# Attention in two layers: score products of 128 rows throughout, two units per step, the sink as a column, keys and queries laid out by their loads

## Chip, cores and metric

The kernel runs on one core of one Trainium2 chip. The metric is device time in microseconds of one execution; a verdict compares medians of runs on the same chip. Before the change the median of three runs is 3075.5 us (3071.46 to 3081.49).

## What is computed

Two transformer layers over 1024 latent tokens and 256 context tokens of width 1024, in float32. Layer 0 mixes tokens by a Fourier transform in half its channels and by windowed attention with a sink in the other half (8 query heads, 2 key heads). Layer 1 is attention over neighbourhoods of a grid with a learned bias (16 heads). Each ends with a SwiGLU layer. Cut to the attention:

```python
def _window_attention(q, k, v, k_ctx, v_ctx, sink):
    s_win = jnp.einsum('bnqkgd,bnjkd->bnkgqj', qb, kw).astype(jnp.float32) * scale
    s_ctx = jnp.einsum('bnqkgd,bjkd->bnkgqj', qb, k_ctx).astype(jnp.float32) * scale
    s_win = jnp.where(mask[None, :, None, None], s_win, NEG)
    p = jax.nn.softmax(jnp.concatenate([s_win, s_ctx, sk], axis=-1), axis=-1).astype(v.dtype)
    o = (jnp.einsum('bnkgqj,bnjkd->bnqkgd', p[..., :nw], vw)
         + jnp.einsum('bnkgqj,bjkd->bnqkgd', p[..., nw:nw + C], v_ctx))
...
def one_row(r):          # layer 1
    s_nb = jnp.einsum('bqhd,bjhd->bhqj', q_row, k_rows).astype(jnp.float32) * scale + bias[None]
    s_nb = jnp.where(mask[None, None], s_nb, NEG)
    s_cx = jnp.einsum('bqhd,bjhd->bhqj', q_row, k_ctx).astype(jnp.float32) * scale
    p = jax.nn.softmax(jnp.concatenate([s_nb, s_cx], axis=-1), axis=-1).astype(v.dtype)
```

`sk` is the sink: one more score per head that enters the sum of the softmax and has no value.

## The kernel before

Products that need float32 accuracy are made of parts: an operand is `hi` + `lo`, two numbers of TensorE's reduced float32 type, and a product is three matmuls (`mm3`, lines 74 to 76). The dense layers are long runs of those.

The attention of both layers goes by **units**: 128 queries of one head with up to 640 keys (three blocks of 128 in the window, two of context), 80 units in layer 0 and 128 in layer 1. The class `Unit` has the steps of one:

- `scores`: a head has 64 features, so a query's `hi` and `lo` are stacked into 128 rows, `q_st`. For each of two runs of keys one product takes `q_st` with `k_st`, the keys' high parts written twice, one in each half of the rows (line 658). A second takes the 64 rows of the queries' high parts with the keys' low parts `k_l` (line 659). The sums go into a two-bank PSUM tile `s_ps`, of which there are two.
- `maxima` (line 592, on DVE): bias or mask added, the maximum taken, `s_ps` read out into `sm`.
- `exponents` (line 598, on ACT): `pr` = exp, with its sum. In layer 0 a second exponential (line 601) makes the sink's part and POOL adds it (line 602).
- `normalise`: the reciprocal on DVE (line 606), the product with it on POOL (line 607).
- `turn` (line 615): TensorE transposes `pr` by blocks of 128 into PSUM banks `pt_ps`; DVE copies the first run of keys out (line 621), ACT the second (line 619).

`values` (lines 714 and 1181) multiplies turned probabilities with the values, each of two heads in 64 columns of the array, into `po`; ACT and DVE `split` the result into `o_hi`, `o_lo` in layer 0 (lines 720, 722) or `h_hi`, `h_lo` in layer 1 (lines 1188, 1190).

`pipeline` writes these steps in a skewed order, a unit at a time: scores of unit i, turn of unit i − 3 or i − 4, the exponential and normalisation of unit i − 1, the maximum of unit i, then values of an earlier pair in four or three parts. In layer 1 that order is binding for PE, DVE, ACT and POOL; in layer 0 a scheduler arranges the instructions from it. Ahead of units in layer 0 stand the steps of `ada_third` (line 149: a 1 MB load of `ada_w` and four products, 40 times), which make later layers' modulation vectors, and `load_q0`, which loads and turns a tile of queries; in layer 1 loads of the next pair of heads and the addition of masks to the bias tables.

In layer 1 keys and queries come from DRAM, where `turn_qk` put them while the in-projection ran: keys in three arrays (high parts twice for each head of a pair, low parts), queries in two. `load_part` (line 1120) brings a pair's keys and queries in on POOL's DMA queue and values on SP's. In layer 0 `turn_keys` (lines 488 to 496) builds `kA`, `kB` (high parts, twice) and `kL` (low parts) in SBUF during the Fourier mixing. Loads and stores on one engine's queue are issued in the order in which they are written.

Of the kernel before, what the change touches and what calls it, by code (L numbers as in the profile page):

```python
# [16 lines left out]
P = 128  # L17
D = 1024
KT = D // P
# [14 lines left out]
class Pools:  # L34
    """Tile pools opened and closed by hand, so that lifetimes need not nest in the source."""
# [20 lines left out]
def bc(ap, axis, n):  # L56
    """The AP with a dimension of stride 0 put in at `axis`."""
    ap = ap.unsqueeze(axis)
    shape = list(ap.shape)
    shape[axis] = n  # L60
    return ap.broadcast_to(shape)


def build(tc, io):
# [7 lines left out]
    def mm3(out, lh, ll, rh, rl, first, last):  # L72
        """out += l^T r with both operands as exact sums of two float32r parts."""
        TE.matmul(out, lh, rh, start=first, stop=False)  # L74
        TE.matmul(out, lh, rl, start=False, stop=False)  # L75
        TE.matmul(out, ll, rh, start=False, stop=last)  # L76

    def rsqrt_into(r, v, tmp):
        """r = v ** -0.5: a table's value and one Newton step."""
# [6 lines left out]
    # ------------------------------------------------------------------ constants  # L86
# [82 lines left out]
    # ------------------------------------------------------------------ DRAM scratch  # L169
# [4 lines left out]
    q1_d = tc.dram_tile([P, 8, 2, 8, P], F32, name="q1_d")  # L174
# [28 lines left out]
    def modulate(hi, lo, x, r, a, b, wk, n, perm=None, shaped=lambda t: t):  # L203
        """hi + lo = x * r * a + b; `perm` reads the tokens in another order."""
# [6 lines left out]
    # ------------------------------------------------------------------ layer 0: in-projection  # L211
# [26 lines left out]
    def rstd0(c, x):  # L238
        """Steps to the roots of a chunk."""
# [38 lines left out]
    # the first chunk takes the modulation vectors and the weights as they arrive  # L278
# [98 lines left out]
    for c in range(T // CH):  # L377
        h_hi, h_lo = hs[c]

        for u in range(CH // P):  # L380
# [10 lines left out]
            if j == NT - 1:  # L391
                # the room of the inputs and of their norms is free for the Fourier mixing
# [19 lines left out]
            # rotation  # L412
# [17 lines left out]
            # queries: (hi | lo) of a pair's first head, (lo | hi) of its second  # L430
# [28 lines left out]
    # twiddle columns: of l1 = 0 and 4 (cos | -sin), 1..3 (cos | -sin | -cos), context 0, 1 (cos | -sin)  # L459
# [8 lines left out]
    def stage_b(ps, a_hi, a_lo, sgn):  # L468
        """cos part +- sin part over channels."""
# [4 lines left out]
    mask = ac.tile([P, 1152], F32, name="mask0")  # L474
# [8 lines left out]
    kL = ac.tile([P, T], F32R, name="kL")  # L483
    kraw = fp.tile([P, NT, P], F32, name="kraw", tag="fx")
    nc.sync.dma_start(kraw, k_d)
    def turn_keys():
        for t0, n in ((0, 4), (4, 4), (8, 2)):
# [5 lines left out]
            for dst, q in ((kA, slice(0, 64)), (kB, slice(64, P))):  # L493
                for o in (slice(0, 64), slice(64, P)):
                    S.activation(dst[o, sl], ps[q, :w], AF.Copy, scale=0.125)
                V.scalar_tensor_tensor(kL[q, sl], ps[q, :w], 0.125, fl(dst[q, sl]), ALU.mult, ALU.subtract)

    for half in range(2):
# [4 lines left out]
        # order of g: l1 = 0, 4, 1 (re, -im), 2 (re, -im), 3 (re, -im)  # L503
# [58 lines left out]
    # ------------------------------------------------------------------ attention units  # L562
    class Unit:
        """Softmax of 128 queries of one head: scores, probabilities, their transpose in two parts.

        `parts` has the blocks of keys in two runs, each in a PSUM bank: (first slot, keys)."""
# [17 lines left out]
        def maxima(self):  # L584
            """Scores with their bias and the opposite of their maximum, both negated."""
            n = self.ncol
            self.sm = self.wk.tile([P, 640], F32, name="sm", bufs=3)
# [7 lines left out]
        def exponents(self):  # L595
            n, st = self.ncol, self.st
            self.pr = self.wk.tile([P, 640], F32, name="pr", bufs=5)
            S.activation(self.pr[:, :n], self.sm[:, :n], AF.Exp, bias=st[:, 0:1], scale=-1.0,  # L598
                         accum_out=st[:, 1:2])
# [24 lines left out]
    def pipeline(units, before, after, lag_turn=2, lag_after=3):  # L624
# [4 lines left out]
        def at(i, *steps):  # L629
            if 0 <= i < n:  # L630
                for f in steps:
                    getattr(units[i], f)()
# [722 lines left out]
```

## Time and profile before

| | us |
|---|---|
| median of three runs | 3075.5 |
| profiled execution, first to last instruction (span) | 3094.0 |
| span from the start to 232: in-projection of layer 0, Fourier mixing | 232 |
| 232 to 503: attention of layer 0 | 271 |
| 503 to 1909: dense layers, in-projection of layer 1 | 1406 |
| 1909 to 2251: attention of layer 1 | 342 |
| 2251 to the end: dense layers | 843 |

The profile was taken in an execution of its own; it gives no other time of that execution than the span. How to read it: PE is the matmul, PEld the load of its stationary operand; a PE entry's duration runs to the modelled end of its result, so entries overlap, and the time from one start to the next is what a product costs in a run of them. A row of the stages (windows) has the stage, its length, then busy time and instruction count of PE, PEld, DVE, ACT and POOL, the granted TensorE clock, the share of the DMA engines and GB/s. A row of groups has line, engine, operation, names, shapes and count, then busy us and mean ns, then idle us of the engine just before, with what ended it. `64*128` ahead of a shape is rows by columns of the array in use. float32 products that are not of the reduced type stand as two entries each.

### The profile page before, as it was taken

To read this page: it belongs to the slowest core of one execution; us is meant where nothing else is said; L and a number is where in the kernel's file an instruction comes from. 1 tells how busy PE (TensorE), PEld (TensorE's weight loads), DVE (VectorE), ACT (ScalarE), POOL (GpSimd) and SP (SyncE) were. 2 spreads that over 40 slices of the span, in tenths; PEclk is the share of its full clock that TensorE was granted. 3 is DMA by queue.
4 is the path that set the end of the run, shared out by engine and by line. 5 is a ranking of instruction groups with operands and counts; after the bars stand their busy time and mean duration, and the time that the engine had idled before them with its cause. 6 is when DMAs were issued, how large, how long until landed. Compare 5 with 4: busy or idle time off the path is not lost.

```text
span 3094.0 us, 37257 instructions
## 1 busy us (share of the span) xinstructions
PE 3030.7 (98%) x14830; PEld 2331.0 (75%) x14830; DVE 1420.0 (46%) x2540; ACT 939.9 (30%) x1793; POOL 323.7 (10%) x451
## 2 busy tenths in 40 slices
PE   7989999999999999999989999999999999999999
PEld 5874556888888888888867887565577888888887
DVE  5773444533223333333577261555556433544446
ACT  4443443331111111111365252455544111111110
POOL 0112222100000000000220002444310000000000
PEclk9997999999999999999999998999999999999999
DMA  7234546210111110111135244233142111111111
GB/s 264 102 128 143 187 160 211 68 48 35 41 35 41 41 39 31 41 41 41 48 109 171 89 128 149 102 119 120 55 150 69 48 35 62 41 55 41 55 41 68
DMA packets 123165, 267.32 MB, mean 86 GB/s; under 512 B 9040, under 2 KB 77136, under 8 KB 113904
## 3 DMA queue, kind: packets, MB, share of 16 engines
q1 hardware_dynamic: 115568, 228.30, 22.0%
q0 software_dynamic: 3248, 28.12, 2.5%
q10 hardware_dynamic: 4176, 8.53, 0.7%
q8 instruction: 117, 1.92, 0.3%
q14 instruction: 56, 0.46, 0.0%
HBM read 218.64 MB, written 46.27 MB: 86 GB/s over the span
## 4 chain that ended last, share of the span: by engine, by line
PE 91%; DVE 4%; ACT 2%; DMA 1%; issue 1%; POOL 1%; SPq 0%; ACTq 0%; POOLq 0%; DVEq 0%
PE d_ps L74 9%; PE d_ps L76 9%; PE d_ps L75 8%; PE u_ps L76 7%; PE u_ps L75 7%; PE u_ps L74 7%; PE g_ps L74 7%; PE g_ps L76 7%; PE g_ps L75 7%; PE pt_ps L615 5%; PE s_ps L659 4%; PE s_ps L658 4%; PE po L1181 3%; PE po L714 2%; PE ada_ps L149 2%; DVE nrm_t L842 1%
## 5 line engine op out<-in xcount | busy, mean ns | idle before, releaser
L790 ACT CAST w_hi<-w_raw 128x1024 fp32r<-128x1024 f32 x188 | 195.5, 1050 | 890.4 <-PE d_ps L75 490.6
L893 DVE SCALAR_TENSOR_TENSOR x<-d_ps,mod,x 128x512 f32<-128x512 f32 (+1 forms) x400 | 348.3, 881 | 166.2 <-PE d_ps L76 165.9
L791 DVE TENSOR_TENSOR w_lo<-w_raw,w_hi 128x1024 fp32r<-128x1024 f32 x184 | 224.0, 1225 | 293.6 <-ACT w_hi L790 289.0
L877 DVE TENSOR_TENSOR sg<-sg,u_ps 128x512 f32<-128x512 f32 (+1 forms) x110 | 69.8, 635 | 571.1 <-PE u_ps L76 571.1
L74 PE MATMUL d_ps<-act_hi,w_hi 128*128 128x512 f32 (+1 forms) x880 | 327.7, 373 | 3.4 <-DVE x L893 3.3
L75 PE MATMUL d_ps<-act_lo,w_hi 128*128 128x512 f32 (+1 forms) x880 | 327.7, 372 | 1.3 <-DVE act_lo L879 1.3
L76 PE MATMUL d_ps<-act_hi,w_lo 128*128 128x512 f32 (+1 forms) x880 | 327.9, 373 | 0.0
L74 PEld LDWEIGHTS d_ps<-act_hi,w_hi 128*128 128x128 f32 x880 | 165.5, 188 | 37.5 <-DVE x L893 5.5
L75 PEld LDWEIGHTS d_ps<-act_lo,w_hi 128*128 128x128 f32 x880 | 165.5, 188 | 32.7 <-DVE act_lo L879 1.8
L75 PE MATMUL u_ps<-o_lo,w_hi 128*128 128x512 f32 (+1 forms) x528 | 189.3, 358 | 0.0
L76 PEld LDWEIGHTS d_ps<-act_hi,w_lo 128*128 128x128 f32 x880 | 165.5, 188 | 31.4
L607 POOL TENSOR_SCALAR pr<-pr,st 128x640 f32<-128x640 f32 (+2 forms) x208 | 156.7, 753 | 309.4 <-DVE st L606 246.5
L76 PE MATMUL u_ps<-o_hi,w_lo 128*128 128x512 f32 (+1 forms) x528 | 189.0, 358 | 0.0
L74 PE MATMUL u_ps<-o_hi,w_hi 128*128 128x512 f32 (+1 forms) x528 | 189.0, 358 | 0.0
L74 PE MATMUL g_ps<-o_hi,w_hi 128*128 128x512 f32 (+1 forms) x528 | 188.2, 357 | 0.0
L75 PE MATMUL g_ps<-o_lo,w_hi 128*128 128x512 f32 (+1 forms) x528 | 188.2, 356 | 0.0
L76 PE MATMUL g_ps<-o_hi,w_lo 128*128 128x512 f32 (+1 forms) x528 | 188.2, 356 | 0.0
L598 ACT ACTIVATE pr<-sm,st 128x640 f32<-128x640 f32 (+2 forms) x208 | 162.7, 782 | 22.9 <-DVE st L592 14.5
L619 ACT COPY pt<-pt_ps 128x256 f32<-128x256 f32 (+1 forms) x192 | 81.8, 426 | 272.3 <-PE pt_ps L615 272.2
L825 POOL TENSOR_TENSOR nrm_ss<-nrm_ss,nrm_sq 128x512 f32<-128x512 f32 (+1 forms) x38 | 48.2, 1269 | 1060.0 <-PE d_ps L76 935.4
L615 PE MATMUL pt_ps<-ident,pr 128*128 128x128 f32 x944 | 158.4, 295 | 0.6 <-DVE mod L161 0.3
L878 ACT CAST act_hi<-sg 128x512 fp32r<-128x512 f32 (+1 forms) x110 | 63.7, 579 | 297.2 <-DVE sg L877 297.2
(263 smaller groups left out, 6163.0 us busy)
## 6 DMA issues: line engine op xcount, KB each, us to landing
ada_w<-ada_w SPq DMA_DIRECT2D x48, 1024.0 KB, 4.8
w_raw<-w_gate SPq DMA_DIRECT2D x44, 512.0 KB, 3.2
w_raw<-w_up SPq DMA_DIRECT2D x44, 512.0 KB, 3.2
w_raw<-w_down SPq DMA_DIRECT2D x44, 512.0 KB, 3.2
w_raw<-w_out SPq DMA_DIRECT2D x32, 512.0 KB, 3.3
kq<-k_d POOLq DMA_DIRECT2D x8, 1920.0 KB, 7.6
w_raw<-w_in SPq DMA_DIRECT2D x24, 512.0 KB, 4.3
k_d<-qk_ab SPq DMA_DIRECT2D x40, 256.0 KB, 2.3
```

The costliest lines, as they stand in the source:

```text
L74: TE.matmul(out, lh, rh, start=first, stop=False)
L75: TE.matmul(out, lh, rl, start=False, stop=False)
L76: TE.matmul(out, ll, rh, start=False, stop=last)
L598: S.activation(self.pr[:, :n], self.sm[:, :n], AF.Exp, bias=st[:, 0:1], scale=-1.0, accum_out=st[:, 1:2])
L607: G.tensor_scalar(self.pr[:, :n], self.pr[:, :n], st[:, 3:4], 0.0, ALU.mult, ALU.add)
L615: TE.transpose(pt[:, b * P:(b + 1) * P], self.pr[:, (b0 + b) * P:(b0 + b + 1) * P], ident)
L658: TE.matmul(s_ps, q_st, k_st[:, keys], start=True, stop=False)
L659: TE.matmul(s_ps, q_st[half], k_l[half, keys], start=False, stop=True)
L790: S.copy(hi, raw)
L791: eng.tensor_tensor(lo, raw, fl(hi), ALU.subtract)
L893: V.scalar_tensor_tensor(xs, self.shaped(ps[:, :n]), vec(l, 5)[:, dt, v:v + 1], xs, ALU.mult, ALU.add)
L1181: TE.matmul(po[64 * e_:64 * e_ + 64, us, :], d["v"][:, kt, 64 * e_:64 * e_ + 64], rhs(d["p", g, e_]), start=i == 0, stop=i == len(steps) - ...
```

## The change

All comments go, which moves line numbers by 3 to 5 (the functions keep their names). What changes:

- The keys' low parts are kept twice, one in each half of the rows (`kLA`, `kLB` in layer 0), so the second score product takes all 128 rows of the queries, too (`scores4` in place of `scores`, lines 627 and 628). It adds the product of the two low parts, which was left out before.
- `pipeline2` works on two units (a block) at a time: scores of both; then for each of the two the normalisation of one unit of the block before, maximum and exponential of a new one, the turn of one from two blocks before. Values come in two parts, a part behind each block. The order is binding in both layers.
- The sink is a column behind the scores in `sm`, copied there by POOL; one exponential takes all.
- PSUM: layer 1 has three banks for turned probabilities instead of two and one for `po` instead of two; layer 0 keeps two and one.
- `turn_qk` writes high and low parts as they come, two arrays, one ACT and one DVE instruction each. The loads of a pair write them twice or side by side: four of 64 partitions for keys, two for queries, all on SP's queue.

```diff
-    k1_d = tc.dram_tile([P, 8, 3, NT, P], F32, name="k1_d")
+    k1_d = tc.dram_tile([P, 8, 2, T], F32, name="k1_d")
...
-            for dst, q in ((kA, slice(0, 64)), (kB, slice(64, P))):
+            for dst, low, q in ((kA, kLA, slice(0, 64)), (kB, kLB, slice(64, P))):
                 for o in (slice(0, 64), slice(64, P)):
                     S.activation(dst[o, sl], ps[q, :w], AF.Copy, scale=0.125)
-                V.scalar_tensor_tensor(kL[q, sl], ps[q, :w], 0.125, fl(dst[q, sl]), ALU.mult, ALU.subtract)
+                for o in (slice(0, 64), slice(64, P)):
+                    V.scalar_tensor_tensor(low[o, sl], ps[q, :w], 0.125, fl(dst[q, sl]), ALU.mult, ALU.subtract)
...
+            if self.sink is not None:
+                G.tensor_copy(self.sm[:, n:n + 1], self.init)
...
-            if self.sink is not None:
-                S.activation(st[:, 2:3], self.sink, AF.Exp, bias=st[:, 0:1], scale=1.0)
-                G.tensor_tensor(st[:, 1:2], st[:, 1:2], st[:, 2:3], ALU.add)
...
+    def scores4(s_ps, q, k_hi, k_lo, keys):
+
+        TE.matmul(s_ps, q, k_hi[:, keys], start=True, stop=False)
+        TE.matmul(s_ps, q, k_lo[:, keys], start=False, stop=True)
+
+    def pipeline2(units, before, after):
...
+            for u in new:
+                u.scores()
+            for i in range(2):
+                for u in old[i:i + 1]:
+                    u.normalise()
+                for u in new[i:i + 1]:
+                    u.maxima()
+                    u.exponents()
+                for u in turned[i:i + 1]:
+                    u.turn()
+            for f in after.get(b, ()):
                 f()
...
-        half = slice(64, P) if second else slice(0, 64)
-        TE.matmul(s_ps, q_st, k_st[:, keys], start=True, stop=False)
-        TE.matmul(s_ps, q_st[half], k_l[half, keys], start=False, stop=True)
...
-    pipeline(units, before, after, 3, 4)
+    with tc.manual_schedule(engines={E.PE, E.DVE, E.Activation, E.Pool}):
+        pipeline2(units, before, after)
...
-    pst, pst_cm = pools.open("pst1", bufs=2, psum=True)
-    psv, psv_cm = pools.open("psv1", bufs=2, psum=True)
+    pst, pst_cm = pools.open("pst1", bufs=3, psum=True)
+    psv, psv_cm = pools.open("psv1", bufs=1, psum=True)
...
-                        loads=[(k, k1_d, G), (q, q1_d, G), (v, v1_d, nc.sync)])
+        pair[pr] = dict(k=k, q=q, v=v, loads=[
+            [(fl(k[o, i]), k_src[:, i]) for i in range(2) for o in halves],
+            [(fl(q[o]), q_src[:, i]) for i, o in enumerate(halves)],
+            [(v, v1_d[:, pr])]])
...
-        dst, src, q = pair[pr]["loads"][i]
-        q.dma_start(dst, src[:, pr])
+        for dst, src in pair[pr]["loads"][i]:
+            nc.sync.dma_start(dst, src)
...
-            n = -(-len(steps) // 3)
+            n = -(-len(steps) // 2)
```

On PE, in the middle of layer 1's attention, two units before the change stand so (`s_ps` are scores from the pair's tile `kq`, `pt_ps` turned probabilities, `po` values):

```order
L658 MATMUL s_ps<-kq 128x256
L659 MATMUL s_ps<-kq 128x256
L658 MATMUL s_ps<-kq 128x384
L659 MATMUL s_ps<-kq 128x384
L615 MATMUL pt_ps<-ident,pr 128x128 x5
L658 MATMUL s_ps<-kq 128x256
L659 MATMUL s_ps<-kq 128x256
L658 MATMUL s_ps<-kq 128x384
L659 MATMUL s_ps<-kq 128x384
L615 MATMUL pt_ps<-ident,pr 128x128 x5
L1181 MATMUL po<-pt,v 64x256 x4
```

And a block after it, at the same place (`k` and `q` are now tiles of their own):

```order
L627 MATMUL s_ps<-k,q 128x256
L628 MATMUL s_ps<-k,q 128x256
L627 MATMUL s_ps<-k,q 128x384
L628 MATMUL s_ps<-k,q 128x384
L627 MATMUL s_ps<-k,q 128x256
L628 MATMUL s_ps<-k,q 128x256
L627 MATMUL s_ps<-k,q 128x384
L628 MATMUL s_ps<-k,q 128x384
L616 MATMUL pt_ps<-ident,pr 128x128 x10
L1185 MATMUL po<-pt,v 64x256 x6
```

Eight score products now stand in a row, then ten transposes, then half the values of an earlier pair. On DVE, the same block after the change (line 596 is the maximum with its read of the accumulated value, 622 the copy of turned probabilities):

```order
L596 ISA sm,st<-s_ps,btab_14260 128x640
L596 ISA st 128x1
L622 COPY pt<-pt_ps 128x256
L607 RECIPROCAL st<-st 128x1
L596 ISA sm,st<-s_ps,btab_14260 128x640
L596 ISA st 128x1
L622 COPY pt<-pt_ps 128x256
L1194 TENSOR_TENSOR h_lo<-po,h_hi 128x256
L607 RECIPROCAL st<-st 128x1
```

Each copy stands behind a maximum of the same block, and `h_lo` ahead of the next block's first reciprocal and maximum. On SP's queue, where the in-projection ends and layer 1's attention begins, the change has:

```order
L1057 DMA k_d<-qk_hi 128x4x128
L1057 DMA k_d<-qk_lo 128x4x128
L1084 DMA v_d<-v_o 128x4x128 x9
L1124 DMA k<-k_d 64x2x1280 x4
L1124 DMA q<-q_d 64x2x1024 x2
L1124 DMA v<-v_d 128x1280
```

Before, the loads of `k` and `q` for the first pair stood on POOL's queue, and behind the nine stores of `v_o` SP had only the load of `v`.

More of the change, by code (lines that the diff above doesn't have):

```diff
@@ L622, in turn @@
                 b0 += n
-    def pipeline(units, before, after, lag_turn=2, lag_after=3):
-        n = len(units)
-        assert all(i < n for i in before)
[L629 to L632, printed above, removed]
-        for i in range(max([n + lag_turn] + [a + 1 + lag_after for a in after])):
-            if i < n:
-                for f in before.get(i, ()):
-                    f()
-                units[i] = units[i]()
-            at(i, "scores")
-            at(i - lag_turn, "turn")
-            at(i - 1, "exponents")
-            at(i, "maxima")
-            at(i - 1, "normalise")
-            for f in after.get(i - lag_after, ()):
+    def scores4(s_ps, q, k_hi, k_lo, keys):
+        TE.matmul(s_ps, q, k_hi[:, keys], start=True, stop=False)
+        TE.matmul(s_ps, q, k_lo[:, keys], start=False, stop=True)
+    def pipeline2(units, before, after):
+        n = len(units) // 2
+        last = max([n + 2] + [a + 1 for a in after])
+        for b in range(last):
+            new, old, turned = (units[2 * i:2 * i + 2] if 0 <= i < n else [] for i in (b, b - 1, b - 2))
+            if b < n:
+                for i in (2 * b, 2 * b + 1):
+                    for f in before.get(i, ()):
+                        f()
+                    units[i] = units[i]()
+                new = units[2 * b:2 * b + 2]
+            for u in new:
[9 more added lines that the diff above has]
+            for f in after.get(b, ()):
                 f()
@@ L653, in build @@
     psa, psa_cm = pools.open("psa", bufs=1, psum=True)
-    def scores(s_ps, second, q_st, k_st, k_l, keys):
-        half = slice(64, P) if second else slice(0, 64)
-        TE.matmul(s_ps, q_st, k_st[:, keys], start=True, stop=False)
-        TE.matmul(s_ps, q_st[half], k_l[half, keys], start=False, stop=True)
     units, before, after = [], {}, {}
@@ L698, in f @@
                 return Unit(aw, pss, pst, bias, nsink[:, h:h + 1], parts, qst["p", j, g][:, e, u],
-                            lambda s_ps, keys: scores(s_ps, g == 1, qst[j][g][:, i * P:(i + 1) * P],
-                                                      kB if g else kA, kL, keys),
+                            lambda s_ps, keys: scores4(s_ps, qst[j][g][:, i * P:(i + 1) * P],
+                                                       kB if g else kA, kLB if g else kLA, keys),
                             sink=sink[:, h:h + 1])
@@ L722, in split @@
                 V.tensor_tensor(lo, qst["po", j, g], fl(hi), ALU.subtract)
-        i0 = len(units)
+        b0 = len(units) // 2
         units.extend(make(u) for u in range(2))
         if e == 1:
-            for i in range(4):
-                after.setdefault(i0 + 1 + i, []).append(lambda i=i: values(i))
             for i in range(2):
-                after.setdefault(i0 + 4 + 1 + 1 * i, []).append(lambda i=i: split(i))
+                after.setdefault(b0 + 3 + i, []).append(lambda i=i: values(i))
+            for i in range(2):
+                after.setdefault(b0 + 4, []).append(lambda i=i: split(i))
     order = (0, 1, 2, 3, 4, 5, 6, 7, 8, 9)
@@ L1042, in turn_qk @@
             TE.transpose(ps[:, i * P:(i + 1) * P], out[:, i * P:(i + 1) * P], ident)
[L1043 removed]
+        hi = dl.wk.tile([P, 512], F32R, name="qk_hi", tag="act_hi")
+        lo = dl.wk.tile([P, 512], F32R, name="qk_lo", tag="act_lo")
         p0 = 4 * (cc % 2)
         if cc < 2:
[L1046 to L1058 removed]
+            S.copy(hi, ps)
+            V.tensor_tensor(lo, ps, fl(hi), ALU.subtract)
+        else:
+            S.activation(hi, ps, AF.Copy, scale=kg[:, 2:3])
+            V.scalar_tensor_tensor(lo, ps, kg[:, 2:3], fl(hi), ALU.mult, ALU.subtract)
+        dst = q1_d if cc < 2 else k1_d
+        for i, t in enumerate((hi, lo)):
+            nc.sync.dma_start(dst[:, p0:p0 + 4, i, j * P:(j + 1) * P], fl(t).rearrange("p (a n) -> p a n", a=4))
     pending = []
@@ L1190, in split @@
                 V.tensor_tensor(lo, src, fl(hi), ALU.subtract)
-        i0 = len(units)
+        b0 = len(units) // 2
         units.extend(make(u) for u in range(2))
         if e == 1:
-            for i in range(3):
-                after.setdefault(i0 + 1 + i, []).append(lambda i=i: values(i))
             for i in range(2):
-                after.setdefault(i0 + 3 + 2 + 1 * i, []).append(lambda i=i: split(i))
+                after.setdefault(b0 + 3 + i, []).append(lambda i=i: values(i))
+            for i in range(2):
+                after.setdefault(b0 + 4, []).append(lambda i=i: split(i))
     load_part(0, 0)
@@ L1222, in build @@
     with tc.manual_schedule(engines={E.PE, E.DVE, E.Activation, E.Pool}):
-        pipeline(units, before, after, 4, 5)
+        pipeline2(units, before, after)
     pools.close(psv_cm, pst_cm, pss_cm, aw_cm, ac_cm, kp_cm)
```

49 lines of the change are left out of this document (18 added, 31 removed).

## The prediction

> **What bounds the kernel now.** I read the page's slices first, then busy time by stage.
>
> ```profile
> PEclk9997999999999999999999998999999999999999
> ...
> 232.00:503.00 271.00, 268.31 (x1385) 135.29 (x1384) 114.46 (x364) 121.56 (x351) 71.71 (x160) 0.92 0.49 170
> 1909.00:2251.00 342.00, 341.29 (x1827) 204.05 (x1825) 175.25 (x543) 168.74 (x418) 142.57 (x198) 0.97 0.30 102
> ...
> PE pt_ps L615 <- DVE pt L621: 0.3, 1, 0.3
> ```
>
> The two attention stages last 271 and 342 us. PE is busy all through them and the waits of PE hold a single 0.3 us entry in layer 1: TensorE bounds both. DVE, ACT and POOL have half of each stage free. But a busy PE need not be streaming columns, so I read starts in the timeline, layer 1 first, then dense products of 512 and of 256 columns.
>
> ```profile
> 2102.31 1.08 PE L1181 MATMUL po<-pt,v 128*64 128x256 f32 x8
> 2103.32 0.38 PE L658 MATMUL s_ps<-kq 128*128 128x256 f32 x1
> 2103.63 0.38 PE L659 MATMUL s_ps<-kq 64*128 64x256 f32 x1
> 2103.95 0.45 PE L658 MATMUL s_ps<-kq 128*128 128x384 f32 x1
> 2104.32 0.43 PE L659 MATMUL s_ps<-kq 64*128 64x384 f32 x1
> 2104.68 0.76 PE L615 MATMUL pt_ps<-ident,pr 128*128 128x128 f32 x5
> 2105.38 0.44 PE L1181 MATMUL po<-pt,v 128*64 128x128 f32 x4
> ...
> 913.53 0.40 PE L76 MATMUL u_ps<-o_hi,w_lo 128*128 128x512 f32 x1
> 913.77 0.28 PE L74 MATMUL g_ps<-o_hi,w_hi 128*128 128x256 f32 x1
> 913.89 0.28 PE L75 MATMUL g_ps<-o_lo,w_hi 128*128 128x256 f32 x1
> ```
>
> From start to start a dense product of 256 columns takes 0.12 us (0.113 over a run of them) and one of 512 takes 0.24, so 384 should take 0.17. The score products, alternating between 128 and 64 rows, take 0.31 to 0.37: each change of row count costs about 0.20. A unit of 640 keys spends 1.36 us on four score products whose columns need 2 × 0.113 + 2 × 0.17 = 0.57. Five transposes take 0.70, of which 0.54 is columns and 0.16 the change into the 64-column value products; eight of those take 0.91 and the way out 0.10.
>
> **Does that account for the stage?** A pair of heads has 16 units, 12 of 640 keys and 4 of 512: 12 × 1.90 + 4 × 1.68 for scores and transposes, 64 value records of 0.113 and 24 of 0.057, and 12 parts × 0.26 for changes: 41 us, times 8 is 330. The clock does the rest:
>
> ```profile
> 234.00:237.00 3.00, 3.00 (x11) 1.82 (x10) 1.44 (x4) 1.14 (x4) 0.06 (x1) 1.00 0.00 0
> 237.00:240.00 3.00, 3.00 (x12) 0.94 (x12) 1.08 (x6) 2.00 (x6) 1.33 (x4) 0.62 0.00 0
> ...
> 232.00:264.00 32.00, 31.76 (x112) 16.86 (x111) 10.25 (x34) 12.01 (x34) 6.95 (x16) 0.63 0.26 87
> 274.00:292.00 18.00, 18.00 (x60) 9.04 (x62) 5.09 (x14) 5.36 (x16) 2.75 (x6) 0.54 0.33 113
> 1914.00:1937.00 23.00, 23.00 (x66) 13.70 (x68) 8.83 (x29) 7.62 (x19) 9.28 (x13) 0.50 0.43 158
> 1937.00:2251.00 314.00, 313.29 (x1748) 187.43 (x1744) 164.16 (x509) 158.79 (x395) 132.60 (x184) 1.00 0.29 97
> ```
>
> At half clock for 23 us, layer 1 loses some 11: 341 against 342 measured. Layer 0 has two such spells, together about 20 us lost.
>
> **The change, scores.** Every score product now has 128 rows, so eight of two units run on without a change: 1.14 us instead of 2.73. Value products come in two parts instead of three or four. Summing PE alone, a pair becomes 27.5 us, layer 1 220 and layer 0 176 (its units plus 40 modulation steps at 1 us, below, and ten query turns). That is the floor. It is not what I take, because PE then overtakes what feeds it.
>
> ```profile
> L598 ACT ACTIVATE pr<-sm,st 128x640 f32<-128x640 f32 x96 | 79.9, 832 | 0.7 <-DVE st L592 0.7
> L592 DVE CUSTOM_DVE_ANT_0 sm<-s_ps,btab 128x640 f32<-128x640 f32 x96 | 78.3, 815 | 1.8 <-POOL pr L607 1.1 <-issue 0.7
> L607 POOL TENSOR_SCALAR pr<-pr,st 128x640 f32<-128x640 f32 x96 | 77.0, 802 | 139.4 <-DVE st L606 121.1 <-PE pt_ps L615 18.3
> L621 DVE COPY pt<-pt_ps 128x256 f32<-128x256 f32 x128 | 54.4, 425 | 98.9 <-PE pt_ps L615 98.2
> L619 ACT COPY pt<-pt_ps 128x384 f32<-128x384 f32 x96 | 46.1, 480 | 126.4 <-PE pt_ps L615 126.4
> L1190 DVE TENSOR_TENSOR h_lo<-po,h_hi 128x256 fp32r<-128x256 f32 x31 | 12.6, 406 | 0.5 <-ACT h_hi L1188 0.5
> L1188 ACT CAST h_hi<-po 128x256 fp32r<-128x256 f32 x32 | 11.6, 362 | 2.0 <-PE po L1181 2.0
> ```
>
> I laid one layer 1 block of two units end to end in the printed order, 0.08 us from one engine to the next. PE: scores 0 to 1.13, first unit's transposes to 1.67, two of the second's to 1.88. A block fills four transpose banks and has three, so the second unit's last three wait for DVE's copy of the first unit. DVE: its maximum starts when the first scores are out, 0.82 to 1.62, then the copy, to 2.04. So the last transposes run 2.12 to 2.44, the change 0.16, values 1.13, the way out 0.10: 3.83 us, against 5.15 now. Every second block ends with `h_hi` and `h_lo`, which stand ahead of the next maximum on DVE and wait for that block's values: they push the next copy back, and the block behind them takes 4.2 to 4.7. Over a pair the eight blocks come to 31.8 us, 4.0 each; 64 of them with the fill make **257**. Bounds: 220 with no wait, 301 if every block took 4.7.
>
> In layer 0 a block also has a modulation step, and only two banks, so the wait is for ACT: maximum, exponential, ACT copy.
>
> ```profile
> 431.94 0.65 PE L714 MATMUL po<-pt,vt 128*64 128x256 f32 x4
> 432.04 0.37 ACT L619 COPY pt<-pt_ps 128x256 f32<-128x256 f32 x1 [2.68 <-PE pt_ps L615]
> 432.26 0.55 DVE L621 COPY pt<-pt_ps 128x384 f32<-128x384 f32 x1
> 432.52 1.06 PE L149 MATMUL ada_ps<-ada_w,csil 128*32 128x512 f32 x8
> 433.51 0.44 PE L658 MATMUL s_ps<-kB,q 128*128 128x384 f32 x1
> ```
>
> Maximum 0.82 to 1.70, exponential to 2.6, copy of 0.37 to 2.99, last two transposes to 3.28, values 0.90 or 1.36 behind a change of 0.16, then 1.0 for the step (433.51 − 432.52) with 0.13 ahead of it: 5.4 or 5.9, and up to 6.9 behind an `o_lo`. 24 interior blocks × 5.9 = 142, the first four with their query load 23, those of j = 7 24, the eight of the context's queries 30, the drain 8: **227**. Bounds: 176, and 248 with 6.9 for each interior block. The sink's second exponential (0.28 on ACT) goes and a POOL copy comes; POOL has 200 of 271 us free, and the copy falls beside the maximum. Without that cover it would be 80 × 0.2 = 16 us.
>
> **The start of layer 1.** The first pair's keys and queries came on POOL's queue at 1869; now they stand on SP's, behind the stores of `v_o`.
>
> ```profile
> 1866.67 43.92 SPq L1085 DMA_DIRECT2D v_d<-v_o  x9
> 1869.02 0.54 POOL L1120 DMA_DIRECT2D kq<-k_d  x1
> ...
> 1872.00:1875.00 3.00, 3.00 (x15) 2.49 (x14) 0.00 (x0) 0.08 (x1) 1.27 (x3) 1.00 1.00 379
> ...
> kq<-k_d POOLq DMA_DIRECT2D x8, 1920.0 KB, 7.6
> ...
> kq<-q_d POOLq DMA_DIRECT2D x8, 1024.0 KB, 6.6
> ```
>
> SP is held until 1910.6. Four loads of 640 KB and two of 512 KB are 3.67 MB; at 379 GB/s that is 9.7 us, with about 2 for issues and landing: first scores near 1922 rather than 1909.4. I add **13**. Bounds: 11 without the 2, and 17 if they took what the two loads of now take to land, 7.6 and 6.6 us, one behind the other and in part larger. Later pairs load a pair ahead, 32 us early, and cost nothing while a load lands inside that. The Trainium skill, "SBUF — State Buffer", section Door 1: The DMA port swizzle, says that 64 partitions on one side reach only eight of sixteen ports. By that rule these half-height loads take about 19 us instead of 9.7 and the result, an estimate, is 10 us later; no row here has such a load.
>
> **Clock.** Both stages begin as sparsely as now, layer 1 after a pause besides. But at half clock PE works without waits (7 us per block), so I expect it to be granted full speed sooner: 14 us in layer 0 and 7 in layer 1, about two thirds of now (bounds 0 and 30, 0 and 15).
>
> **Small edits.** Low parts of layer 0's keys are written twice:
>
> ```profile
> L496 DVE SCALAR_TENSOR_TENSOR kL<-pt_ps,kA x3: 418/674/683, 203.4 to 216.5; 64x512 fp32r<-64x512 f32 x2, 64x256 fp32r<-64x256 f32 x1
> ...
> 196.00:220.00 24.00, 16.24 (x82) 14.55 (x81) 18.55 (x32) 14.60 (x26) 4.83 (x3) 0.79 0.22 77
> ...
> L1042 PE MATMUL pmisc<-ident,qkv_o 128*128 128x128 f32 x144 | 22.1, 276 | 5.0 <-DVE qk_ab L1048 2.1 <-DVE k_l L1056 1.6 <-DVE qkv_o L1080 1.0
> ```
>
> Six more of these (4 × 0.68 + 2 × 0.42 = 3.6) fall where DVE is the busiest engine and PE idles a third: **+4**, bounds 0 and 5. In layer 1's projection the copies behind the turn of queries and keys shrink from four or six to two; PE waited 3.7 us on them: **−3**, bounds −4 and 0. One DMA fewer per key tile has PE's dense products over it.
>
> **Sum**, against the profile's span of 3094.0: layer 0 227 + 14 = 241 for 271, −30; layer 1 257 + 13 + 7 = 277 for 342, −65; +4 − 3. That is −94, 3000. The span is 18.5 above the median of the runs, 3075.5; taken off there, **2982**.
>
> **Rivals.**
> - *PE alone bounds* (for it: half of every other engine is free; against: the walk above, three or two banks). 220 + 20 and 176 + 14: −183, 2892; anything above half of that lies in 2880 to 2945. 12%.
> - *Half clock returns inside layer 0.* Full speed went when streaming filled about 41% (11 products of 256 columns in 3 us, row 234), and held at 62% (25.4 of 41 us a pair, row 1937). The new blocks stream 80% in layer 1 but 69% in layer 0, with pauses of 0.7 us in it. If layer 0 spent half its blocks at half clock it would take near 290: 3015 to 3066. 12%.
> - *Slower, the clock in both stages.* The mechanism is the same, and decides where the streamed share falls under a point between 41 and 62%. With every product doubled I lay 358 and 424 us: 3075.5 + 87 + 82 + 13 + 1 = 3258. 5%. The Trainium skill, "TensorE: Matmul & The Clock Gate", section Part 4: PE-mode transpose, says transposes do not engage the full clock. By that rule the share without them is 57% in layer 1 and about 53% in layer 0, nearer the point; the steady stretch of now speaks against it, 42% without transposes (17.3 of 41 us) at clock 1.00 (row 1937).
> - *The change does not do what it says*: the 0.20 us is not the row count but the pair of products. Then scores keep 1.36 and the same blocks make 339 and 269: +30 with the pause, 3105, slower. Against it: the dense rows reload weights at each product and lose nothing. 6%.
> - Within 0.3% of now by a mixture: 3%.
>
> **How the numbers follow.** The forecast, 2945 to 3015, has 62%. The range 2915 to 3050 takes in much of the two neighbours and leaves out a fifth. About 0.3% is what a measurement of this kernel can tell from no change: under 3066 lie 62 + 12 + 12 = 86%, within it 3%, above it 11%.
>
> **What would show it.** Score products at 0.11 and 0.17 us start to start; in layer 1 PE waiting on DVE's copy, in layer 0 on ACT's; a first score product of layer 1 some 13 us behind the last projection product, with DMA as its releaser; half clock only in the first 20 us of a stage. Wrong it would be if the products keep 0.31, if PEclk shows 0.5 late in a stage, or if PE waits for loads in later pairs.

## The result, and the profile after

Four runs of the changed kernel take 2993.7 to 2994.9 us, median 2994.1, beside 3078.5 for four of the kernel before: ratio 0.9725, 95% interval 0.9683 to 0.9766. Faster, by 84 us in the medians; the forecast was 2982 with a range of 2915 to 3050. The profiled execution's span is 2991.7 us, 102.3 less than that of before.

First the granted clock by slices (40 equal ones) of the changed kernel:

```profile
PEclk9989999999999999999999999899999999999999
```

Then its stages by windows, in the columns known from before (length, then busy time of PE, PEld, DVE, ACT and POOL, clock, DMA share, GB/s):

```profile
237.00:468.00 231.00, 193.67 (x1368) 114.89 (x1364) 109.30 (x363) 102.53 (x268) 67.13 (x158) 0.99 0.57 203
...
253.00:259.00 6.00, 4.63 (x23) 3.32 (x23) 1.75 (x5) 1.59 (x6) 0.63 (x3) 0.72 0.85 320
456.00:464.00 8.00, 6.81 (x38) 4.20 (x36) 5.14 (x26) 2.66 (x9) 3.23 (x10) 0.79 0.13 37
1874.00:1890.00 16.00, 0.00 (x0) 0.00 (x0) 0.00 (x0) 0.00 (x0) 0.00 (x0) 0.50 1.03 212
1891.00:1897.00 6.00, 5.99 (x21) 4.93 (x22) 3.54 (x12) 2.81 (x7) 2.20 (x4) 0.50 1.06 303
1891.00:2148.00 257.00, 242.39 (x1824) 183.82 (x1824) 159.63 (x544) 163.60 (x417) 133.52 (x184) 0.99 0.64 153
```

PE is no longer busy all through: it idles for 231 − 194 = 37 us in layer 0's attention and for 257 − 242 = 15 in layer 1's, and for a pause ahead of layer 1, in which only DMA moves. The clock is low for a few us at a stage's start and at layer 0's end; before it was low for about 40 us in layer 0 and 23 in layer 1. The score products follow each other so, in the middle of layer 1:

```profile
2003.78 0.28 PE L628 MATMUL s_ps<-k,q 128*128 128x256 f32 x1
2003.89 0.34 PE L627 MATMUL s_ps<-k,q 128*128 128x384 f32 x1
2004.07 0.33 PE L628 MATMUL s_ps<-k,q 128*128 128x384 f32 x1
2004.24 0.28 PE L627 MATMUL s_ps<-k,q 128*128 128x256 f32 x1
```

From start to start it is 0.11 us behind 256 columns and 0.17 to 0.18 behind 384; it was 0.31 and 0.37. To compare stages exactly I take them from the first score product to the first product of the out-projection behind them, by the instructions of the tiles `s_ps` and `d_ps` (the last pair of numbers: first and last start):

```profile
L627 PE MATMUL s_ps<-kA,q x72: 276/286/689, 237.2 to 452.3; 128*128 128x256 f32 x48, 128*128 128x384 f32 x24
L74 PE MATMUL d_ps<-o_hi,w_hi x192: 276/393/501, 468.6 to 582.4; 128*128 128x512 f32 x128, 128*128 128x256 f32 x64
L627 PE MATMUL s_ps<-k,q x256: 274/337/582, 1891.0 to 2135.3; 128*128 128x256 f32 x128
L74 PE MATMUL d_ps<-h_hi,w_hi x128: 393/394/693, 2148.5 to 2241.9; 128*128 128x512 f32 x128
```

So layer 0's attention is 237.2 to 468.6, layer 1's 1891.0 to 2148.5. The same four starts in the profiled execution of every kernel in this study give the stages, in us; the last column is the median of its runs:

| kernel | up to layer 0's scores | layer 0 attention | between | layer 1 attention | median time |
|---|---|---|---|---|---|
| before | 233.7 | 270.4 | 1405.3 | 342.6 | 3078.5 |
| after | 237.2 | 231.4 | 1422.4 | 257.5 | 2994.1 |
| half rows again | 237.6 | 282.7 | 1420.8 | 349.8 | 3138.9 |
| old order | 237.1 | 205.6 | 1423.2 | 243.0 | 2951.9 |
| loads on POOL's queue | 238.6 | 231.3 | 1401.6 | 259.5 | 2973.7 |
| halves apart | 238.3 | 228.0 | 1420.6 | 257.2 | 2989.7 |
| halves together | 236.8 | 230.9 | 1417.7 | 257.2 | 2993.6 |
| two banks | 241.8 | 229.9 | 1427.5 | 308.5 | 3046.1 |
| second exponential | 239.0 | 231.9 | 1421.5 | 257.8 | 2994.5 |
| turns apart | 239.2 | 229.3 | 1422.7 | 257.2 | 2992.3 |
| turn first | 240.2 | 226.0 | 1424.9 | 259.4 | 2991.0 |
| three places | 238.5 | 216.1 | 1404.7 | 243.9 | 2950.8 |
| old order, POOL's queue | 236.5 | 205.1 | 1400.5 | 245.3 | 2933.6 |
| the same, two value parts | 237.6 | 206.6 | 1404.4 | 245.4 | 2936.5 |

Now the pause, in the timeline of the changed kernel, SP's queue and PE:

```profile
1848.53 22.12 SPq L1084 DMA_DIRECT2D v_d<-v_o  x5
1870.81 2.74 SPq L1124 DMA_DIRECT2D k<-k_d  x4
1873.66 1.23 SPq L1124 DMA_DIRECT2D q<-q_d  x2
...
1869.21 0.39 PE L76 MATMUL g_ps<-w_hi,o_lo 128*128 128x512 f32 x1
1891.01 0.55 PE L627 MATMUL s_ps<-k,q 128*128 128x256 f32 x1 [21.42 <-DMA q<-q_d]
```

The loads are issued at 1870.8, right behind the last store of `v_o` and about 1 us behind PE's last projection product, and PE stands for 21.4 us until the last of them has landed. Inside the stages, PE's waits are few and short (us in total, times, longest), four rows of layer 0 and then one of layer 1:

```profile
PE pt_ps L616 <- DVE st L607: 16.1, 32, 0.6
PE ada_ps L149 <- DMA ada_w<-ada_w: 7.5, 6, 2.1
PE pt_ps L616 <- ACT pt L620: 6.3, 26, 0.5
PE pt_ps L157 <- ACT ada_rows L154: 3.9, 5, 2.0
...
PE pt_ps L616 <- DVE pt L622: 10.0, 22, 0.7
```

### The profile page after: what moved, and what is told of

The parts are those of the page before. It is cut to its first block, busy times and chain, and to the rows that moved or that the text cites. A ratio compares the mean times of both kernels' runs of the same rounds, so it can differ in the third digit from the quotient of the medians.

```text
span 2991.7 us, 37131 instructions
## 1 busy us (share of the span) xinstructions
PE 2854.2 (95%) x14830; PEld 2288.4 (76%) x14830; DVE 1372.8 (46%) x2510; ACT 863.2 (29%) x1637; POOL 308.6 (10%) x435
## 4 chain that ended last, share of the span: by engine, by line
PE 73%; DVE 5%; ACT 2%; issue 2%; DMA 2%; POOL 1%; SPq 0%; POOLq 0%; ACTq 0%; DVEq 0%
PE d_ps L76 9%; PE d_ps L74 9%; PE d_ps L75 9%; PE u_ps L76 7%; PE u_ps L75 7%; PE u_ps L74 7%; PE g_ps L76 7%; PE g_ps L74 7%; PE g_ps L75 7%; PE pt_ps L616 1%; DVE sm L596 1%; PE po L1185 1%; DVE nrm_t L846 1%; ACT pr L602 1%; POOL pr L608 1%
## 5 line engine op out<-in xcount | busy, mean ns | idle before, releaser
L602 ACT ACTIVATE pr<-sm,st 128x640 f32<-128x640 f32 (+4 forms) x208 | 162.4, 781 | 224.5 <-DVE st L596 201.5
L616 PE MATMUL pt_ps<-ident,pr 128*128 128x128 f32 x944 | 148.4, 281 | 36.0 <-DVE st L607 16.1
L616 PEld LDWEIGHTS pt_ps<-ident,pr 128*128 128x128 f32 x944 | 105.5, 141 | 68.5 <-DVE pt L622 26.5
```

The source lines that it names most:

```text
L616: TE.transpose(pt[:, b * P:(b + 1) * P], self.pr[:, (b0 + b) * P:(b0 + b + 1) * P], ident)
```

## The experiments

Times are medians of four or five runs each (two for the halves together), beside runs of the kernel before on the same chip. The runs were made in four groups on different chips; the medians of the kernel before in them are 3073.9 to 3081.0, so a difference of less than some 7 us between kernels of different groups is not read as one. A stage is measured as in the table above.

### Half rows again

```diff
-    def scores4(s_ps, q, k_hi, k_lo, keys):
+    def scores4(s_ps, q, k_hi, k_lo, keys, half=slice(0, 64)):
...
-        TE.matmul(s_ps, q, k_lo[:, keys], start=False, stop=True)
+        TE.matmul(s_ps, q[half], k_lo[half, keys], start=False, stop=True)
...
```

> The changed kernel, but the second score product of each run of keys takes 64 rows again (the low part of the queries times the low part of the keys is not added). Theory (each change of row count costs PE about 0.20 us): score products start 0.31 to 0.37 us apart, the layer 1 stage goes from 257 to about 339 us and the layer 0 stage from 231 to about 269; 2994 + 82 + 38 = 3114, 3085 to 3130. Rival (the gain came from the order, units two at a time, and not from the rows): products stay 0.11 to 0.17 apart and the time is 2984 to 3010.

Measured: 3138.9 us, 1.0205 of before (1.0179 to 1.0231). Its score products, in the timeline of layer 1:

```profile
2101.82 0.38 PE L627 MATMUL s_ps<-k,q 128*128 128x256 f32 x1
2102.13 0.38 PE L628 MATMUL s_ps<-k,q 64*128 64x256 f32 x1
2102.44 0.44 PE L627 MATMUL s_ps<-k,q 128*128 128x384 f32 x1
2102.81 0.44 PE L628 MATMUL s_ps<-k,q 64*128 64x384 f32 x1
2103.18 0.38 PE L627 MATMUL s_ps<-k,q 128*128 128x256 f32 x1
```

They start 0.31 to 0.37 us apart again, as in the kernel before, though the instruction has half the rows. The mechanism of the theory holds and the size is a little larger: 349.8 − 257.5 = 92 us in layer 1 where 82 were expected, 51 in layer 0 where 38 were. The granted clock is part of it. The two stages by windows:

```profile
237.60:520.30 282.70, 258.05 (x1368) 133.89 (x1364) 113.06 (x363) 106.12 (x269) 67.07 (x158) 0.92 0.47 167
1941.10:2290.90 349.80, 345.89 (x1825) 210.00 (x1825) 166.53 (x545) 175.62 (x418) 133.38 (x184) 0.96 0.47 113
```

By the means of 0.92 and 0.96 some 23 and 14 us are lost at a low clock, where the changed kernel loses about 3 in each stage; the expectation had no term for that. So by pairs the 128 rows save time in two ways, in the products and in the clock. What was not expected: by pairs and with 64 rows the kernel is **slower than before** in both stages (282.7 against 270.4, 349.8 against 342.6) and in the median (3138.9 against 3076.0, of which the pause is 21). The new order, then, is no help by itself.

### The old order

```diff
-    with tc.manual_schedule(engines={E.PE, E.DVE, E.Activation, E.Pool}):
-        pipeline2(units, before, after)
+    pipeline(units, before, after, 3, 4)
...
-    pst, pst_cm = pools.open("pst1", bufs=3, psum=True)
-    psv, psv_cm = pools.open("psv1", bufs=1, psum=True)
+    pst, pst_cm = pools.open("pst1", bufs=2, psum=True)
+    psv, psv_cm = pools.open("psv1", bufs=2, psum=True)
```

In layer 1 `pipeline(units, before, after, 4, 5)` stands under the binding order, as before; in layer 0 the scheduler arranges the instructions again, as before. The parts of the values are four and three again.

> The changed kernel with its 128-row score products and its loads, but units one at a time in the order, the value parts and the transpose banks of the kernel before. Theory (the rows carry the gain, the order little): PE alone would need some 228 us in layer 1 against 220 for pairs; 2970 to 3030, nearest 3000. Rival (without eight score products in a row the gain is lost): products stay 0.3 apart, 3060 to 3110.

Measured: 2951.9 us, below the theory's range, and 42 us faster than the change. Beside the profiled execution of before, rows alone are worth 270.4 − 205.6 = 65 us in layer 0 and 342.6 − 243.0 = 100 in layer 1; the order by pairs costs 26 and 15 of it. Some 29 us of the 164 are clock (0.92 and 0.97 there, 1.00 and 0.99 here), and that execution's clock was lower than in most others, as shown further down; by medians the rows are worth some 140 (the best version, below). The two windows show where the pairs' loss is:

```profile
237.00:442.00 205.00, 201.08 (x1372) 116.01 (x1372) 115.09 (x363) 107.08 (x270) 70.12 (x157) 1.00 0.64 229
1866.00:2108.00 242.00, 241.02 (x1824) 178.75 (x1824) 170.63 (x544) 165.94 (x417) 133.93 (x184) 0.99 0.69 161
```

PE is busy for all but 4 and 1 us, where by pairs it idles for 37 and 15. The pairs' loss is the idle time that they brought. In layer 0 the binding order came with them, so the 26 us there stand for both.

### Loads on POOL's queue

```diff
-            nc.sync.dma_start(dst, src)
+            q.dma_start(dst, src)
...
-    load_part(0, 0)
-    load_part(0, 1)
+    load_part(0, 0, G)
+    load_part(0, 1, G)
```

> The changed kernel, but the six loads of the first pair's keys and queries are issued from POOL's queue. Theory (PE's pause of 21.4 us ahead of layer 1 is only the time that the loads stand behind the stores of v_o and then take): first score product within 2 us of the last projection product, 2994 - 21 = 2973, 2968 to 2980. Rival (something else that is ready at the same time, the copies or the release of the room, holds PE): 2988 to 2996.

Measured: 2973.7 us. The dense part in between is 20.8 us shorter, the pause is gone (the first score product starts 0.6 us behind the start of the last projection product), and layer 1's stage is 2 us longer. The loads were late, and nothing else was.

### Halves apart, halves together

```diff
-        for dst, src in pair[pr]["loads"][i]:
-            nc.sync.dma_start(dst, src)
+        for n, (dst, src) in enumerate(pair[pr]["loads"][i]):
+            q = nc.scalar if pr == 0 and n % 2 else nc.sync
+            q.dma_start(dst, src)
```

and, in the second, `(n // 2 if i == 0 else n)` in place of `n % 2`.

> The changed kernel, but of the first pair's six loads the three into the upper 64 partitions are issued from ACT's queue, the three into the lower from SP's as before. Theory (loads into one half of the partitions reach half of the way into SBUF, so lower and upper at a time run at twice the rate): some 380 GB/s instead of 215, 10 us of loading instead of 19, PE's pause 12 us instead of 21.4, time 2985. Rival (a row of 5 KB for 64 partitions is slow whatever runs beside it): 215 GB/s, pause 21, time 2994.

> The changed kernel with the first pair's loads on two queues as in the run with the halves apart, but of the keys each queue writes the lower 64 partitions first and then the upper ones, so that both queues write into one half at a time; of the queries SP has the lower, ACT the upper half. Theory (one half of the partitions takes 215 GB/s, whoever writes): 205 to 225 GB/s for the keys, 266 to 295 for the queries, pause 19 to 21 us. Rival (two queues were faster, not two halves): 266 to 295 GB/s from the start, pause 17 to 19.

Measured: pauses of 18.9 and 19.8 us, times of 2989.7 and 2993.6. What was moved, first with the halves apart, while both queues worked and when one was left, then the same with the halves together, then the rate of loads into 128 partitions in the changed kernel:

```profile
1872.00:1882.00 10.00, 0.00 (x0) 0.00 (x0) 0.00 (x0) 0.00 (x0) 0.00 (x0) 0.50 1.03 279
1882.00:1886.00 4.00, 0.00 (x0) 0.00 (x0) 0.00 (x0) 0.00 (x0) 0.00 (x0) 0.50 1.03 211
```

```profile
1870.00:1878.00 8.00, 0.00 (x0) 0.00 (x0) 0.00 (x0) 0.00 (x0) 0.00 (x0) 0.50 1.04 274
1878.00:1884.00 6.00, 0.00 (x0) 0.00 (x0) 0.00 (x0) 0.00 (x0) 0.00 (x0) 0.50 1.05 209
```

```profile
1892.00:1894.00 2.00, 2.00 (x9) 1.65 (x8) 1.29 (x3) 0.81 (x2) 0.00 (x0) 0.50 1.10 396
```

With the halves apart neither theory nor rival held: 279 GB/s is neither 380 nor 215. With the halves together the rate was the rival's, 274, and the pause the theory's, 19.8, because 209 followed as soon as one queue was left. Two queues raise the rate from 212 to 274–279 GB/s whichever halves they were meant to fill, which speaks against the halves. Whether the two queues kept in step in the second run can't be seen in the records, so the cause of 212 stays open. Rows of 5 KB alone are not the cause: the row of 396 is the load of `v`, rows of 5 KB into 128 partitions, and the bias tables' behind it; from 1894 to 1896, with the next pair's loads into 64 partitions, the rate is 222 again.

### Two banks

```diff
-    pst, pst_cm = pools.open("pst1", bufs=3, psum=True)
+    pst, pst_cm = pools.open("pst1", bufs=2, psum=True)
```

> The changed kernel with two transpose banks in layer 1 instead of three. Theory (a block of two units turns into four banks, and PE waits for the copies that free them): the walk gives 305 us for the layer 1 stage instead of 257, so 2994 + 48 = 3042, 3020 to 3060. Rival (banks hardly matter: PE's waits there add up to 11 us): below 3005.

Measured: 3046.1 us, layer 1's stage 308.5, where the prediction's way of walking a block, with two banks, gave 305. Banks are what a block by pairs waits for. The old order has two banks and no such wait.

### Second exponential

```diff
-            if self.sink is not None:
-                G.tensor_copy(self.sm[:, n:n + 1], self.init)
...
+            if self.sink is not None:
+                S.activation(st[:, 2:3], self.sink, AF.Exp, bias=st[:, 0:1], scale=1.0)
+                G.tensor_tensor(st[:, 1:2], st[:, 1:2], st[:, 2:3], ALU.add)
```

> The changed kernel, but the sink is no column of the scores: a second exponential of one column on ACT and an addition on POOL, as in the kernel before; POOL's copy of the sink is gone. Theory (the sink's form costs nothing in either way): layer 0 stage 231 us and 2991 to 2998. Rival 1 (ACT sets the pace of layer 0): 80 exponentials of 0.28 us, up to 22 us more, 3016. Rival 2 (ACT's 16.5 us of waits for POOL's copy are real): up to 16 us less, 2978.

Measured: 2994.5 us, layer 0's stage 231.9. The sink as a column changes nothing that these runs can tell.

### What the order by pairs waits for: turns apart, turn first

A block of the changed kernel in the timeline, behind the end of a group (`h_lo`):

```profile
2004.71 0.93 PE L616 MATMUL pt_ps<-ident,pr 128*128 128x128 f32 x7
...
2004.75 0.42 DVE L1194 TENSOR_TENSOR h_lo<-po,h_hi 128x256 fp32r<-128x256 f32 x1 [1.40 <-ACT h_hi L1192]
...
2005.16 0.80 DVE L596 CUSTOM_DVE_ANT_0 sm<-s_ps,btab 128x640 f32<-128x640 f32 x1
...
2005.89 0.42 DVE L622 COPY pt<-pt_ps 128x256 f32<-128x256 f32 x1
...
2006.37 0.55 PE L616 MATMUL pt_ps<-ident,pr 128*128 128x128 f32 x3 [0.73 <-DVE pt L622]
```

PE's last three transposes need the bank that DVE's copy frees, and ahead of the copy stand `h_lo`, which has waited for ACT, and a maximum. First only PE's order was changed, the scores of a unit and then a turn, twice:

```diff
-            for u in new:
-                u.scores()
             for i in range(2):
+                for u in new[i:i + 1]:
+                    u.scores()
```

> The changed kernel, but PE takes the scores of the first unit, its turn, the scores of the second, its turn, instead of both scores and then both turns; the other engines keep their order. Theory (what the order by pairs costs is PE's idle time in front of transposes whose banks are not free): layer 0 stage 231 to about 210 us, layer 1 from 257 to about 245, time 2960, 2950 to 2970. Rival (eight score products in a row are worth something, or the wait comes from elsewhere in the block): 2988 to 3010.

Measured: 2992.3 us, the stages 229.3 and 257.2. The theory failed: on DVE the copy still stands behind the maximum, and PE waits 10.8 us for it in layer 1, as before the edit (10.0). Then only the other engines' order, with the turn ahead of normalisation, maximum and exponential in the loop:

> The changed kernel by pairs, but within a block the turn of a unit is written ahead of the maximum and the exponential of the new one, as the old order had it: on DVE and ACT the copies that free the transpose banks no longer stand behind work that waits for the new scores. Theory (this place in the queues of DVE and ACT is what the order by pairs costs; moving PE's transposes alone left the wait as it was): layer 1 stage from 257 to about 245 us, layer 0 from 231 to about 210, time 2994 - 12 - 21 = 2961, 2952 to 2970. Rival (the pairs themselves cost it, by scores that now wait for both maxima of the block before): 2985 to 3000.

Measured: 2991.0 us, the stages 226.0 and 259.4. The theory failed as well. The timeline shows what is late next, first in layer 0, then in layer 1:

```profile
301.24 0.71 PE L616 MATMUL pt_ps<-ident,pr 128*128 128x128 f32 x5
...
301.99 0.37 ACT L620 COPY pt<-pt_ps 128x256 f32<-128x256 f32 x1 [1.85 <-PE pt_ps L616]
...
302.50 0.74 PE L616 MATMUL pt_ps<-ident,pr 128*128 128x128 f32 x5 [0.55 <-ACT pt L620]
...
2006.96 0.36 ACT L1192 CAST h_hi<-po 128x256 fp32r<-128x256 f32 x1
2007.35 0.42 DVE L1194 TENSOR_TENSOR h_lo<-po,h_hi 128x256 fp32r<-128x256 f32 x1 [1.36 <-ACT h_hi L1192]
2007.44 0.48 ACT L620 COPY pt<-pt_ps 128x384 f32<-128x384 f32 x1
2007.69 0.42 DVE L622 COPY pt<-pt_ps 128x256 f32<-128x256 f32 x1
...
2007.97 0.55 PE L616 MATMUL pt_ps<-ident,pr 128*128 128x128 f32 x3 [0.41 <-ACT pt L620]
```

In layer 0 the copies now begin at once, but the second turn follows the first without a score product in between, and with two banks it must wait for the copies themselves. In layer 1 both copies stand behind the group's output, ACT's behind `h_hi` and DVE's behind `h_lo`, which waits for `h_hi`. The last three transposes now start behind ACT's copy and ahead of the end of DVE's, so the wait has moved: PE waits 11.4 us on ACT's copy in this stage and no longer on DVE's. Each mend leaves other waits at nearly the same place.

### Three places at once

The turn behind its own unit's scores on PE, ahead of the maximum on DVE and ACT, and the second half of `split` in the middle of the next block; the first loads on POOL's queue:

```diff
-            for u in new:
-                u.scores()
             for i in range(2):
+                for u in new[i:i + 1]:
+                    u.scores()
+                for u in turned[i:i + 1]:
+                    u.turn()
                 for u in old[i:i + 1]:
                     u.normalise()
...
-                for u in turned[i:i + 1]:
-                    u.turn()
+                for f in after.get(b - 0.5, ()) if i == 0 else ():
+                    f()
...
-                after.setdefault(b0 + 4, []).append(lambda i=i: split(i))
+                after.setdefault(b0 + 4 + 0.5 * i, []).append(lambda i=i: split(i))
```

> The order by pairs with three places mended together, and the first pair's loads on POOL's queue: PE takes scores and turn of one unit, then of the other; copies of a turn stand ahead of the new maximum and exponential on DVE and ACT; the second half of a group's output (h_lo, o_lo) stands on DVE in the middle of the next block and not behind h_hi or o_hi at once. Theory (PE's idle time by pairs is 37 us in layer 0 and 15 in layer 1, and these three waits cover for one another, so that mending one alone shows nothing): layer 0 stage 231 to 205 or less, layer 1 257 to 245 or less, time 2994 - 21 - 26 - 12 = 2935, as with the old order, 2925 to 2942. Rival (pairs cost by something else, such as maxima and exponentials that come two at a time): at least 2955. If the layer 1 stage alone keeps 257, h_lo is not what it waits for.

Measured: 2950.8 us, between the two. In layer 1 the theory held: 243.9 us, as in the old order, so these places together make up what the pairs cost there (which of them would do alone was not run beyond the two above). PE still waits 8.2 us in that stage for `h_lo`, which holds the one `po` bank. In layer 0 it went from 231.4 to 216.1, 15 of the 26 us. PE's waits that are left there:

```profile
PE pt_ps L157 <- ACT ada_rows L154: 9.7, 5, 2.5
PE ada_ps L149 <- DMA ada_w<-ada_w: 7.5, 4, 3.2
PE po L719 <- DVE o_lo L727: 6.8, 16, 1.1
```

They belong to the modulation steps, which stand two at a time ahead of a pair, and to `o_lo`. The granted clock is lower, too: 0.98 in this stage against 1.00 in the old order, by which some 4 of the 10 us that are left are clock (an estimate). That the waits make up the rest is a reading of this view; it was not tried, and neither was the scheduler's order with pairs.

### The best version

The old order with the 128-row products and the first loads on POOL's queue:

> 128-row score products in the old order of units, and the first pair's keys and queries from POOL's queue. Theory (the two gains lie at different places and add up): 2952 - 21 = 2931, 2926 to 2937. Rival (without the pause the half clock or the loads of later pairs give part of it back): 2938 to 2950.

Measured: **2933.6 us**, 0.9538 of before (0.9508 to 0.9569) and 60 us less than the change. The two gains add up. One more step, value products in two parts (`-(-len(steps) // 2)`, `-(-len(keys) // 2)` and two entries of `after` for three or four):

> The old order with 128-row scores and the first loads on POOL's queue (2933.6), and the value products in two parts instead of three or four. Theory (each part costs PE two changes, 0.26 us together, and PE is busy all through): 32 parts fewer in layer 1 and 20 in layer 0, 13 us less, 2920, 2915 to 2926. Rival (longer runs of value products hold up the scores and the gain is lost in waits): 2930 to 2945.

Measured: 2936.5 us, no gain: its stages are as long as without. The 13 us, worked out from 0.26 per part, were not there to be had.

## Why the prediction was right, and where it was off

Its terms, against the two profiled executions:

| step of the prediction | predicted | measured |
|---|---|---|
| `turn_keys`, up to the first scores | +4 | +3.5 |
| layer 0: 271 to 227 + 14 | −30 | −39.0 |
| `turn_qk`, dense part without the pause | −3 | 1401.0 − 1405.3 = −4.3 |
| start of layer 1 | +13 | +21.4 |
| layer 1: 342 to 257 + 7 | −78 | −85.1 |
| behind layer 1 | 0 | +1.2 |
| sum | −94 | −102.3 |

- **The scores were right.** The price of a change of row count carried the forecast, and the half rows bring it back. The rival that the change doesn't do what it says is out.
- **The walks were right.** With the clock's loss taken off (6 × 0.28 + 8 × 0.21 = 3.4 us in layer 0, 6 × 0.50 = 3 in layer 1) the stages are 228 and 254.5; predicted were 227 and 257. In layer 1 PE waits on DVE's copy, as said. In layer 0 the view names ACT's copy for 6.3 us and DVE's reciprocal for 16.1; a reciprocal frees no bank. A block shows what it stands for:

```profile
302.99 0.56 DVE L622 COPY pt<-pt_ps 128x384 f32<-128x384 f32 x1
303.46 0.15 DVE L607 RECIPROCAL st<-st 128x1 f32<-128x1 f32 x1
303.69 0.52 PE L616 MATMUL pt_ps<-ident,pr 128*128 128x128 f32 x3 [0.52 <-DVE st L607]
...
304.01 0.35 ACT L620 COPY pt<-pt_ps 128x256 f32<-128x256 f32 x1
304.42 0.44 PE L616 MATMUL pt_ps<-ident,pr 128*128 128x128 f32 x2 [0.21 <-ACT pt L620]
```

The second unit's turn waits twice: three transposes for the bank that DVE's copy frees, right ahead of the reciprocal, then two for ACT's copy. ACT's copy ends last, as said; that PE stops for DVE's before it, and for longer, the prediction did not say.

- **What the prediction missed about the order.** It took the waits of a block as the price of PE overtaking the others. With the same products a unit at a time there is nearly no wait (4 and 1 us of idle time). The floor of 220 and 176 was not reached by any kernel here; PE alone is busy for 241 and 201 us in the old order, 242 and 194 by pairs. That "eight of two units run on without a change" is true, but four products of one unit, followed by its neighbour's transposes, which have 128 rows, too, run on as well.
- **The start of layer 1 was mis-sized**: +13, bounds 11 to 17, measured 21.4. The rate of 379 GB/s was that of loads into 128 partitions; these moved at 212. The Trainium skill, "SBUF — State Buffer", section Door 1: The DMA port swizzle, by which 64 partitions on one side reach eight of sixteen ports, gave about 19 us of loading, an estimate, and the trace is near the amount: 3.67 MB at 212 GB/s are 17.3 us. The two runs with two queues don't decide whether its reason holds.
- **The clock was mis-sized**: 14 and 7 us lost, measured 3.4 and 3. That full speed returns sooner was right in direction. In the attention stages, behind their starts, the clock fell back once, to 0.50 from 457 to 460 at the end of layer 0, where PE's work thins out; that is the 0.79 of the row 456 to 464 and cost 1.7 us. Both rivals on the clock, which had it over half of the blocks or all of them, are out. (In the second of them the streamed share of layer 1 without transposes, 57%, doesn't follow from its rows: 17.3 of 31.8 us are 54%.)
- **The step that moved the number most was the last one**: "The span is 18.5 above the median of the runs, 3075.5; taken off there". The changed kernel's profiled span is 2.4 us *below* its median (in every run here the time is about 2 us more than the span). Thirty further executions of the kernel before show what the 18.5 was: they go from 3069.7 us at a mean granted clock of 0.993 to 3090.2 at 0.985, in nearly the order of their clocks, and span times clock is the same in all of them within 0.3% (3039 to 3047). The profiled one had 0.983. Its excess over the median was time at a low clock. Where in the execution is not shown, as only this one has a trace; but the dense layers behind layer 1 have none of it (842.0 us in it and in the best version) and those between the stages at most 5 (1405.3 against 1400.5), which leaves the attention stages, where some 31 us were lost. Of these the sum had already taken 10 away in its clock terms (31 to 14 + 7) when it took off 18.5, and the changed kernel loses only 6.4.
- **Part of the nearness is luck.** The errors of the sum are −14.6 in the clock, +8.4 at the start of layer 1 and −2.1 in all other terms, together −8; the last step makes +21. So errors of up to 21 us cancel to the 12 by which 2994 lies above 2982.

## What to carry to other kernels

When a change bundles a cheaper instruction with a new order, price the order by itself, with the cheaper instruction in the old order as the rival: here the rows were worth some 140 us in medians (3073.9 to 2933.6, with the small edits), and the pairs took 42 back (2994.1 against 2951.9). A wait for a buffer can have several covers: mend one and another ends at the same time, so read what is late next before judging a mend by its time. And if the profiled execution is slow because of its clock, take its excess off once: in the clock's terms or at the end.

## What the runs showed of the hardware

- A product of 64 rows between products of 128 costs more than the 128-row product that replaces it: 0.31 us from start to start against 0.11 to 0.12 at 256 columns.
- Loads into 64 partitions moved 212 GB/s from one queue and 274 to 279 from two, with the DMA engines shown fully busy in either case, while loads into 128 partitions moved up to 396.
- The spread of the kernel before over thirty executions, 3069.7 to 3090.2 us, is a spread of the granted clock: 0.993 to 0.985, nearly in that order.
- By pairs, products of 64 rows go with a lower granted clock: four runs had a mean of 0.976 to 0.981 with them and four 0.989 or 0.990 without. That the spread goes with them is not shown: two kernels without them, with two banks and with the halves together, still spread over 11 and 14 us.
